# Low parts of 36 last-layer weights, made in the SwiGLU before and read back from DRAM, in place of GpSimd subtractions

## The chip, the core and the metric

The program runs on one core of one Trainium2 chip. A core has TensorE (PE in the profile, with its weight loads as PEld), VectorE (DVE), ScalarE (ACT), GpSimd (POOL) and SyncE (SP), which here issues DMAs, and 16 DMA engines that move data between DRAM and the on-chip SBUF. Every engine works through its own list of instructions in order; an instruction waits until the semaphores that it names have been raised. The metric is the device time of one execution in microseconds (us).

## The reference

Two layers of a block with four token mixers side by side, on 256 latent and 256 context tokens, width 1024, in float32. What matters here, cut down:

```
for l in range(2):
    x = x + 0.5 * g1 * swiglu(modulate(rms_norm(x), sh1, sc1), w_gate, w_up, w_down)   # both layers: latent and context
    y, yc = token_mixers(...)              # MLA, GLA, GQA, Hyena; then
    #   y = (sum over branches i of sigmoid(u @ w_gates_i) * (out_i @ w_branch[i])) @ w_out
    x = x + g2 * y
    x = x + 0.5 * g3 * swiglu(modulate(rms_norm(x), sh3, sc3), ...)                    # layer 1: latent tokens only
return rms_norm(x) * final_g
```

Hyena takes its three inputs from `u @ w_dp` (1024 to 1536 columns, 12 tiles of 128). The branch gates take `u @ w_gates` (4 x 1024 columns, 32 tiles of 128), the branch products `out_i @ w_branch[i]` (512 to 1024).

## The kernel before

**Split arithmetic.** A float32 product is made of three reduced ones. Each weight tile (128 partitions x 1024 float32, 512 KB) is loaded by SP into one of three raw buffers `wr` (`raw`, L318). `pieces` (L328) cuts it into two pieces of 512 columns. For each piece ScalarE writes the rounded high part `wh` (L311) and a second engine writes the rest, `wl = wr - wh` (L312). There are 8 buffers of each, so four weights can lie split ahead of TensorE. `mm3` (L303) then issues three matmuls per 128-column block: `wh` with the high part of the activation, `wh` with its low part, `wl` with its high part. The subtraction runs on VectorE, except where `self.share` is set: there GpSimd makes it (L335).

**Stages.** Layer 0 ends with its second SwiGLU on all 512 tokens (`ffn`, L586, called at L1408): three groups of 8, 8 and 6 hidden tiles, in each first the gate and up products (`gu`, two weights per hidden tile), then eight `dn` products. After each hidden tile or `dn` tile `side()` runs one step of other work; here that is 16 rows of the next layer's modulation (`ada_rows`, L453: one 512 KB load and two VectorE products with the conditioning row). Layer 1 runs its first SwiGLU, then the mixers for 256 latent tokens (`mixer`, L1339): first MLA and GQA, woven with the projections (`prep`). Then comes **the stage of this change** (L1357): Hyena and GLA are woven as two chains of high priority, and the merges of branches 0 (MLA) and 2 (GQA) fill in between them. Its weights are 12 `w_dp` tiles (for the three Hyena inputs, L1188), 8 `w_br` and 16 `w_gate` tiles (L1299, L1303), 36 in all, 72 pieces. In this stage `share` is 1, so all 72 subtractions are GpSimd's. The merges of branches 3 and 1 and the output product follow, with VectorE subtractions.

**What sets the order.** A tile scheduler fixes the order of each engine's instructions when the program is built, from priorities (`first`, `evac`, `ahead`) and its own costs. Pools hand out buffers in rotation; a tile that takes a buffer over waits for its last reader. SP's DMAs stand in one list, so a DMA that waits holds up those behind it.

Of the kernel before, what the change touches and what calls it, by code (L numbers as in the profile page):

```python
# [8 lines left out]
F32 = mybir.dt.float32  # L9
F32R = mybir.dt.float32r  # L10
# [7 lines left out]
P = 128  # L18
D = 1024
KD = 8  # L20
L = 256
NT = 512
DEPTH = 2
# [31 lines left out]
AHEAD = 200  # L55
EVAC = 400

SHARE_W = 1


PHASES = {"first": {"fh": 11, "fl": 9, "hp": 8, "aw": 6, "cb": 2},
# [158 lines left out]
class Net:  # L220
    def __init__(self, ctx, tc, A, out):
        self.tc, self.nc, self.A, self.out = tc, tc.nc, A, out
        pool = lambda n, b, **k: ctx.enter_context(tc.tile_pool(name=n, bufs=b, **k))
        self.const = pool("const", 1)
        self.sm = pool("sm", 2)
        self.up = pool("up", 1)
        self.wr = pool("wr", 3)
        self.wh = pool("wh", 8)
        self.wl = pool("wl", 8)
        self.fixed = {k: pool(k, b) for k, b in (("t", 6), ("m", 3), ("v", 8))}  # L230
        self.acc = (pool("acc0", 2, space=PSUM), pool("acc1", 2, space=PSUM))
        self.sps = pool("sps", 2, space=PSUM)
        self.tps = pool("tps", 2, space=PSUM)
        self.scopes = [ctx.enter_context(ExitStack()), ctx.enter_context(ExitStack())]
        self.dram = pool("dr", 1, space=bass.MemoryType.DRAM)
        self.mod = {}
        self.ahead = 0
        self.piece = 0
        self.share = 0
        self.begun = []  # L240

    def phase(self, name, sub=None):
# [77 lines left out]
        self.nc.sync.dma_start(out=r[:rows, :n], in_=ap)  # L320
        return r

    def weights(self, ap, n, rows=P, piece=512):

        with self.tc.high_priority(offset=-self.ahead):
            return self.pieces(self.raw(ap, n, rows), n, rows, min(piece, n))

    def pieces(self, r, n, rows, piece):  # L328
        parts = []
        for o in range(0, n, piece):  # L330
            m = min(piece, n - o)
            h = self.wh.tile([P, 512], F32R, tag="wh", name="wh")
            l = self.wl.tile([P, 512], F32R, tag="wl", name="wl")
            self.piece += 1
            eng = self.nc.gpsimd if self.share and self.piece % self.share == 0 else None  # L335
            self.two(h[:rows, :m], l[:rows, :m], r[:rows, o:o + m], eng)
            parts.append((h, l))

        def at(c, m):
            h, l = parts[c // piece]  # L340
            c %= piece
            return h[:rows, c:c + m], l[:rows, c:c + m]

        return at
# [238 lines left out]
            self.fm(p, w, u, n, ks=range(KD // 2))  # L583
            self.begun.append((w, p))

    def ffn(self, l, f, u, n, gt, filler=(), rows=()):  # L586
        nc, A = self.nc, self.A
        filler = list(filler)
        rows = self.rows(rows)

        def side():
            if filler:
                filler.pop(0)()
            else:
                next(rows, 0)

        for g0, g1 in GROUPS:
            hs = []
            for j in range(g0, g1):
                ps = []  # L600
                for e in range(2):
                    if self.begun:
                        w, p = self.begun.pop(0)
                        self.fm(p, w, u, n, ks=range(KD // 2, KD))
                    else:
                        w = self.weights(A["gu"][l, f, j, e], 1024)
                        p = self.psa(e, "gu")
                        self.fm(p, w, u, n)
                    ps.append(p)
                t = self.t("ft")  # L610
                nc.scalar.activation(t[:, :n], ps[0][:, :n], AF.Tanh, scale=0.5)
                nc.vector.scalar_tensor_tensor(out=t[:, :n], in0=t[:, :n], scalar=1.0, in1=ps[0][:, :n],
                                               op0=ALU.add, op1=ALU.mult)
                nc.vector.tensor_mul(t[:, :n], t[:, :n], ps[1][:, :n])
                h, lo = self.pair("fh", "hh", n, "fl")
                self.two(h[:, :n], lo[:, :n], t[:, :n])
                hs.append((h, lo))
                side()
            if gt.__class__ is tuple:
                gt = self.gate(*gt)  # L620
            q = g1 - g0
            for m in range(KD):
                w = self.weights(A["dn"][l, f, m, :, g0 * P:g1 * P], q * P)
                p = self.psa(m % 2, "dn")
                for j in range(q):
                    self.mm3(p[:, :n], w(j * P, P), (hs[j][0][:, :n], hs[j][1][:, :n]),
                             j == 0, j == q - 1)
                self.resid(p, m, n, gt)
                side()
        for _ in rows:  # L630
            pass

    def rows(self, pairs):
        if pairs:
            self.crow = [self.ld(self.tl("cb", "crow", D), self.cb[s]) for s in range(2)]
        for l, i in pairs:
            yield from self.ada_rows(l, i)

    def resid(self, p, m, n, gt):
        for s in range(n // L):  # L640
# [541 lines left out]
    def hyena(self, l, u, nseq, out):  # L1182
        nc, A = self.nc, self.A
        n = nseq * L

        def conv(i, z):
            p = self.psa(1, "dp")
            self.fm(p, self.weights(A["w_dp"][l, i], 1024), u, n)  # L1188
            w = [self.v["sw"][:, l * 36 + j * 12 + i:l * 36 + j * 12 + i + 1] for j in range(3)]
            nc.scalar.activation(z[:, :n], p[:, :n], AF.Identity, scale=w[1],  # L1190
                                 bias=self.v["sb"][:, l * 12 + i:l * 12 + i + 1])
            z3, p3 = (x[:, :n].rearrange("p (s t) -> p s t", t=L) for x in (z, p))
            nc.vector.scalar_tensor_tensor(out=z3[:, :, 1:], in0=p3[:, :, :L - 1], scalar=w[0], in1=z3[:, :, 1:],
                                           op0=ALU.mult, op1=ALU.add)
            nc.vector.scalar_tensor_tensor(out=z3[:, :, :L - 1], in0=p3[:, :, 1:], scalar=w[2], in1=z3[:, :, :L - 1],
                                           op0=ALU.mult, op1=ALU.add)

        src = self.packed("hv", "hv", n, 4)
# [10 lines left out]
        for i in range(2 * nseq):  # L1209
# [3 lines left out]
            h, lo = self.tl("o", "zth", 512, F32R), self.tl("o", "ztl", 512, F32R)  # L1213
# [3 lines left out]
        for od in range(2):  # L1217
# [6 lines left out]
            if od:  # L1224
                dst = [self.pair("o", "od", n) for _ in range(4)]
            nz = []
            for s in range(nseq):

                z = []
                for e in range(2):  # L1230
                    p = [self.half(F, 2 * e + k, zt[2 * s + k], "Z") for k in range(2)]
# [9 lines left out]
                a, b, c, d = z  # L1241
# [52 lines left out]
    def merge(self, l, b, ob, u, n, first=False, last=None):  # L1294
        nc, A = self.nc, self.A
        if first:
            self.y = self.packed("y", "y", n, KD)
        for mp in range(4):
            wb = self.weights(A["w_br"][l, b, mp], 1024)  # L1299
            for e in range(2):  # L1300
                m = 2 * mp + e
                pg = self.psa(0, "gate")
                self.fm(pg, self.weights(A["w_gate"][l, b * KD + m], 1024), u, n)  # L1303
                t = self.tl("m", "mt")
                if n == NT:
                    nc.scalar.activation(t[:, :n], pg[:, :n], AF.Tanh, scale=0.5)
                    p = self.psa(1, "br")
                else:
                    p = pg[:, n:]
                for k in range(4):  # L1310
                    self.mm3(p[:, :n], wb(e * 512 + k * P, P), (ob[k][0][:, :n], ob[k][1][:, :n]), k == 0, k == 3)
                with self.evac():
                    if n < NT:
                        nc.scalar.activation(t[:, :n], pg[:, :n], AF.Tanh, scale=0.5)
                    y = self.y[m]
                    nc.vector.scalar_tensor_tensor(out=y if first else t[:, :n], in0=t[:, :n], scalar=1.0, in1=p[:, :n],  # L1316
                                                   op0=ALU.add, op1=ALU.mult)
                    if not first:
                        nc.vector.tensor_add(y, y, t[:, :n])  # L1319
                if last is not None:  # L1320
                    h, lo = self.pair("yh", "yh", n, "yl")
                    self.two(h[:, :n], lo[:, :n], y)
                    last.append((h, lo))
                yield
# [14 lines left out]
    def mixer(self, l, u, last):  # L1339
# [4 lines left out]
        if last:  # L1344
# [3 lines left out]
                next(prep)  # L1348
            self.weave([self.mla(l, nq, oa), self.gqa(l, nq, oc)], prep)
            self.phase("end", "end2")  # L1350
            self.share = SHARE_W

            def merges():
                yield from self.merge(l, 0, oa, u, n, first=True)
                yield from self.merge(l, 2, oc, u, n)

            self.weave([self.hyena(l, u, nseq, od), self.gla(l, nq, ob)], merges())  # L1357
            self.share = 0
            for _ in self.merge(l, 3, od, u, n):
                pass  # L1360
        else:
# [14 lines left out]
    def run(self):  # L1376
# [14 lines left out]
        for l in range(DEPTH):  # L1391
# [13 lines left out]
            self.phase("ffn")  # L1405
            u = self.norm(*self.gain(l, 2), n)
            self.ada(l, 8)
            self.ffn(l, 1, u, n, (l, 2, 0.25), (), [] if last else later(l + 1, 0, 1))  # L1408
            if not last:
                u = self.norm(*self.gain(l + 1, 0), NT)  # L1410
        self.norm(self.v["final_g"], None, L)
# [21 lines left out]
```

## Time and profile before

| | |
|---|---|
| median of three runs | 2608.75 us (lowest 2604.82) |
| profiled execution | 2601.85 us, its span 2600.1 us |
| PE busy | 2497.5 us, 96% of the span |
| DVE, ACT, POOL busy | 1696.6, 1091.1, 264.9 us |
| DMA | 369.01 MB, mean 142 GB/s, 42.8% of 16 engines |
| TensorE's granted clock, mean | 0.986 |

The page cuts the span into 40 slices of 65 us. The second SwiGLU of layer 0 fills about 1173 to 1505 us, slices 18 to 23; the stage of the change about 2053 to 2292 us, slices 31 to 35. A digit is a busy share in tenths. All DMAs of the program were issued by SP (queue q1, `hardware_dynamic`); POOL issued none.

### The profile page before, as it was taken

Reading aid. Unit: us, or ns where it says so; the run is one execution under the profiler, and the core shown is the slowest. Engines: PE = TensorE matmul, PEld = TensorE weight load, DVE = VectorE, ACT = ScalarE, POOL = GpSimd, SP = SyncE. Lnnn points to the kernel's source line nnn. Section 1 sums busy time; section 2 is a strip of 40 time slices with the busy share of each in tenths; the row PEclk is TensorE's granted clock in tenths of the full one; section 3 lists DMA queues with packets and bytes.
Section 4 is the critical chain, followed back from the end, with each engine's and each line's share of the span. In section 5 each row is a group of like instructions: output and inputs, shape, how many; then the busy total and the mean of one; then the engine's idle time right before and its main releaser. Section 6 shows DMA issues by size and latency. Waiting matters only on the chain. (4 is left out here: it accounts for less than half of the span.)

```text
span 2600.1 us, 36866 instructions
## 1 busy us (share of the span) xinstructions
PE 2497.5 (96%) x13624; PEld 2058.8 (79%) x13624; DVE 1696.6 (65%) x3377; ACT 1091.1 (42%) x2127; POOL 264.9 (10%) x240
## 2 busy tenths in 40 slices
PE   6999999999999999999999999999999987899998
PEld 4778887887877667777888878888888777788998
DVE  5667858577547778746744466767458667776665
ACT  4333223333545554433232343232346664455554
POOL 2110003001000000020000030000020147401000
PEclk9999999999999999999999999999999999899999
DMA  7564535332313123245623244545353333356554
GB/s 253 176 213 170 190 128 192 134 108 100 126 57 122 61 88 106 89 156 174 205 97 97 86 158 146 178 146 174 102 187 130 114 120 122 114 161 210 177 184 124
DMA packets 122371, 369.01 MB, mean 142 GB/s; under 512 B 14090, under 2 KB 19660, under 8 KB 122192
## 3 DMA queue, kind: packets, MB, share of 16 engines
q1 hardware_dynamic: 122192, 366.66, 42.8%
q8 instruction: 107, 1.75, 0.3%
q14 instruction: 72, 0.59, 0.1%
HBM read 346.16 MB, written 20.45 MB: 141 GB/s over the span
## 5 line engine op out<-in xcount | busy, mean ns | idle before, releaser
L311 ACT CAST wh<-wr 128x512 fp32r<-128x512 f32 (+1 forms) x926 | 564.0, 613 | 1070.3 <-PE gu L301 396.0
L312 DVE TENSOR_TENSOR wl<-wr,wh 128x512 fp32r<-128x512 f32 (+1 forms) x854 | 577.1, 682 | 410.1 <-ACT wh L311 399.3
L301 PE MATMUL gu<-ul,wh 128*128 128x512 f32 (+1 forms) x1408 | 514.7, 366 | 2.5 <-DVE ul L542 2.5
L301 PE MATMUL gu<-uh,wh 128*128 128x512 f32 (+1 forms) x1408 | 512.3, 366 | 2.4 <-ACT uh L536 2.3
L301 PE MATMUL gu<-uh,wl 128*128 128x512 f32 (+1 forms) x1408 | 511.5, 364 | 1.3 <-DVE wl L312 1.3
L301 PE MATMUL dn<-hh,wh 128*128 128x512 f32 (+1 forms) x1408 | 389.5, 363 | 0.0
L301 PEld LDWEIGHTS gu<-ul,wh 128*128 128x128 f32 x1408 | 265.7, 189 | 58.4 <-DVE ul L542 9.3
L301 PEld LDWEIGHTS gu<-uh,wh 128*128 128x128 f32 x1408 | 265.8, 189 | 52.0 <-ACT uh L536 7.2
L301 PEld LDWEIGHTS gu<-uh,wl 128*128 128x128 f32 x1408 | 265.6, 189 | 44.0 <-DVE wl L312 1.7
L301 PEld LDWEIGHTS dn<-hh,wh 128*128 128x128 f32 x1408 | 252.6, 188 | 41.3
L301 PE MATMUL dn<-hh,wl 128*128 128x512 f32 (+1 forms) x704 | 255.3, 363 | 0.0
L502 POOL TENSOR_TENSOR nacc<-nacc,sq 128x512 f32<-128x512 f32 (+1 forms) x39 | 46.2, 1185 | 1745.1 <-ACT sq L500 1736.7
L301 PE MATMUL gate<-uh,wh 128*128 128x256 f32 (+1 forms) x768 | 202.3, 328 | 3.3 <-DVE y L1316 3.3
L464 DVE SCALAR_TENSOR_TENSOR aj<-aw,crow 128x1024 bf16<-128x1024 f32 x160 | 193.7, 1224 | 0.0
L301 PE MATMUL gate<-uh,wl 128*128 128x512 f32 (+1 forms) x512 | 177.0, 346 | 4.3 <-POOL wl L312 2.8
L301 PEld LDWEIGHTS dn<-hh,wl 128*128 128x128 f32 x704 | 132.3, 188 | 20.4
L301 PEld LDWEIGHTS gate<-uh,wh 128*128 128x128 f32 x768 | 132.0, 195 | 15.4 <-DVE y L1316 3.5
L301 PE MATMUL tm<-wh,uh 128*128 128x256 f32 x576 | 140.3, 288 | 1.6 <-ACT uh L536 1.0
L312 POOL TENSOR_TENSOR wl<-wr,wh 128x512 fp32r<-128x512 f32 x72 | 106.4, 1489 | 239.9 <-ACT wh L311 234.1
L301 PE MATMUL tm<-wl,uh 128*128 128x256 f32 x432 | 124.1, 287 | 0.0
L301 PEld LDWEIGHTS gate<-uh,wl 128*128 128x128 f32 x512 | 99.1, 194 | 15.9 <-POOL wl L312 3.0
L642 DVE SCALAR_TENSOR_TENSOR x<-dn,gt,x 128x256 f32<-128x256 f32 x168 | 74.4, 478 | 54.6 <-PE dn L301 54.6
(408 smaller groups left out, 3975.7 us busy)
## 6 DMA issues: line engine op xcount, KB each, us to landing
wr<-in_gu SPq DMA_DIRECT2D x176, 512.0 KB, 3.5
aw<-in_adat SPq DMA_DIRECT2D x80, 512.0 KB, 3.6
wr<-in_dn SPq DMA_DIRECT2D x64, 512.0 KB, 3.6
wr<-in_w_gate SPq DMA_DIRECT2D x64, 512.0 KB, 3.5
aw<-in_ada SPq DMA_DIRECT2D x48, 512.0 KB, 4.6
wr<-in_w_tm SPq DMA_DIRECT2D x36, 512.0 KB, 3.6
wr<-in_w_br SPq DMA_DIRECT2D x32, 512.0 KB, 3.5
wr<-in_dn SPq DMA_DIRECT2D x32, 384.0 KB, 3.2
```

Of the source, the lines that this page charges most:

```text
L301: self.nc.tensor.matmul(out, l, r, start=start, stop=stop)
L311: self.nc.scalar.copy(h, src)
L312: (eng or self.nc.vector).tensor_sub(l, src, h)
L464: nc.vector.scalar_tensor_tensor(out=x, in0=w, scalar=1.0, in1=self.crow[s], op0=ALU.mult, op1=ALU.mult, accum_out=o[:, s:s + 1])
L502: (nc.vector if first and k % 2 else nc.gpsimd).tensor_add(acc[:, :n], acc[:, :n], sq[:, :n])
L642: self.nc.vector.scalar_tensor_tensor(out=self.x[m][:, c], in0=p[:, c], scalar=gt[:, m, s:s + 1], in1=self.x[m][:, c], op0=ALU.mult, op1=A ...
```

## The change

`LOWS` lists the 36 weights of the stage, in the order in which they are needed. In layer 0's second SwiGLU each step of `side()` also runs `low_part` for one of them: SP loads the weight into a 1024-column buffer of the pool `aw` (5 buffers, shared with the modulation rows), ScalarE and VectorE split it as usual, and SP stores the two low pieces (256 KB each) to a DRAM tile. In the `dn` half of a group `side()` leaves the modulation rows alone as long as weights remain in the list. In the stage, `pieces` still loads the raw weight and lets ScalarE make `wh`; `wl` is now filled by a DMA that GpSimd issues from the DRAM tile. GpSimd's subtractions are gone, with `share` and `SHARE_W`.

```diff
+L1 = DEPTH - 1
+LOWS = tuple([(L1, "w_dp", i) for i in (8, 9, 10, 11)]
+             + [k for mp in range(4) for k in ((L1, "w_br", 0, mp), (L1, "w_gate", 2 * mp), (L1, "w_gate", 2 * mp + 1))]
+             + [(L1, "w_dp", i) for i in range(8)]
+             + [k for mp in range(4) for k in ((L1, "w_br", 2, mp), (L1, "w_gate", 16 + 2 * mp),
+                                               (L1, "w_gate", 17 + 2 * mp))])
...
-    def pieces(self, r, n, rows, piece):
+    def pieces(self, r, n, rows, piece, low=None):
         parts = []
         for o in range(0, n, piece):
             m = min(piece, n - o)
             h = self.wh.tile([P, 512], F32R, tag="wh", name="wh")
             l = self.wl.tile([P, 512], F32R, tag="wl", name="wl")
-            self.piece += 1
-            eng = self.nc.gpsimd if self.share and self.piece % self.share == 0 else None
-            self.two(h[:rows, :m], l[:rows, :m], r[:rows, o:o + m], eng)
+            if low is not None:
+                self.nc.scalar.copy(h[:rows, :m], r[:rows, o:o + m])
+                self.nc.gpsimd.dma_start(out=l[:rows, :m], in_=low[:rows, o:o + m])
+            else:
+                self.two(h[:rows, :m], l[:rows, :m], r[:rows, o:o + m])
             parts.append((h, l))
...
-        def side():
+        def side(low_only=False):
             if filler:
                 filler.pop(0)()
-            else:
+            elif not (low_only and lows):
                 next(rows, 0)
+            if lows:
+                self.low_part(lows.pop(0))
...
                 self.resid(p, m, n, gt)
-                side()
+                side(True)
...
+    def low_part(self, key):
+        src = self.A[key[1]][(key[0], *key[2:])]
+        w = self.ld(self.tl("aw", "lw", 1024), src)
+        dst = self.low[key] = self.dram.tile([P, 1024], F32, name="low" + "_".join(str(x) for x in key))
+        for o in (0, 512):
+            h, lo = self.t("lwh", F32R), self.t("lwl")
+            self.two(h, lo, w[:, o:o + 512])
+            self.nc.sync.dma_start(out=dst[:, o:o + 512], in_=lo)
...
-            self.fm(p, self.weights(A["w_dp"][l, i], 1024), u, n)
+            self.fm(p, self.weights(A["w_dp"][l, i], 1024, key=(l, "w_dp", i)), u, n)
...
-            self.share = SHARE_W
...
-            self.share = 0
...
-            self.ffn(l, 1, u, n, (l, 2, 0.25), (), [] if last else later(l + 1, 0, 1))
+            self.ffn(l, 1, u, n, (l, 2, 0.25), (), [] if last else later(l + 1, 0, 1), () if last else LOWS)
```

How the scheduler lays it out is seen at three places. First **GpSimd's list in the stage**, before (`yv` is a product of Hyena, `wl<-wr,wh` a subtraction):

```order
L763 MEMSET krp 128x64 x4
L312 TENSOR_TENSOR wl<-wr,wh 128x512 x48
L1245 TENSOR_TENSOR yv<-za,H 128x512
L1245 TENSOR_TENSOR yv<-zb,H 128x512
L312 TENSOR_TENSOR wl<-wr,wh 128x512 x24
L1245 TENSOR_TENSOR yv<-za,H 128x512
L1245 TENSOR_TENSOR yv<-zb,H 128x512
```

and with the change (the start of the stage, and the rows around its first `yv`):

```order
L782 MEMSET krp 128x64 x4
L341 DMA wl<-low_w_dp_10975 128x512 x2
L341 DMA wl<-low_w_br_0_11367 128x512 x2
L341 DMA wl<-low_w_gate_11465 128x512 x2
...
L341 DMA wl<-low_w_gate_12947 128x512 x2
L341 DMA wl<-low_w_gate_12997 128x512 x2
L1264 TENSOR_TENSOR yv<-za,H 128x512
L1264 TENSOR_TENSOR yv<-zb,H 128x512
L341 DMA wl<-low_w_dp_12553 128x512 x2
```

72 DMA issues stand where 72 subtractions stood; 46 of them, where 48 were, come ahead of the first `yv`.

Second, **SP's list in the SwiGLU**, at the end of the first group's `gu` products, before:

```order
L320 DMA wr<-in_dn 128x1024
L289 DMA aw<-in_adat 128x1024
L320 DMA wr<-in_dn 128x1024 x2
L289 DMA aw<-in_adat 128x1024
L320 DMA wr<-in_dn 128x1024 x2
```

and with the change:

```order
L324 DMA wr<-in_dn 128x1024
L293 DMA lw<-in_w_br 128x1024
L656 DMA low_w_gate_11465<-lwl 128x512 x2
L293 DMA lw<-in_w_gate 128x1024
L324 DMA wr<-in_dn 128x1024 x2
L293 DMA lw<-in_w_gate 128x1024
L656 DMA low_w_gate_11563<-lwl 128x512 x2
L293 DMA lw<-in_w_br 128x1024
L324 DMA wr<-in_dn 128x1024 x2
```

Between the loads of the SwiGLU's own weights (`wr`) now stand loads and stores of the low parts; a store waits for VectorE's `lwl`, and the next `wr` load stands behind it.

Third, **ScalarE's list at the last hidden tile of the first group**, with the change (`ft` and `hh` belong to the hidden tile, `lwh` to a low part):

```order
L620 ACTIVATE ft<-gu 128x512
L315 CAST lwh<-lw 128x512
L315 CAST wh<-wr 128x512
L315 CAST lwh<-lw 128x512 x3
L315 CAST wh<-wr 128x512
L315 CAST hh<-ft 128x512
L315 CAST lwh<-lw 128x512
L315 CAST wh<-wr 128x512
L315 CAST lwh<-lw 128x512 x3
L315 CAST wh<-wr 128x512
L315 CAST lwh<-lw 128x512 x4
```

Before, the same piece was `ft`, two casts of `wh`, `hh`, and 18 casts of `wh` in a row. Four casts of low parts now stand between `ft` and `hh`, and the low parts of the `dn` half crowd at its beginning. TensorE's own list is the same up to the late mixers; from there on gates and Hyena products come in another order.

## Rows read from the trace of the kernel before

**Rows 1.** The page: busy time of TensorE, and its granted clock in tenths, 40 slices.

```profile
PE 2497.5 (96%) x13624; PEld 2058.8 (79%) x13624; DVE 1696.6 (65%) x3377; ACT 1091.1 (42%) x2127; POOL 264.9 (10%) x240
PEclk9999999999999999999999999999999999899999
```

**Rows 2.** Busy time by stretch; last columns: granted clock, DMA share, GB/s.

```profile
core 0: us, PE busy (x) PEld busy (x) DVE busy (x) ACT busy (x) POOL busy (x), PEclk, DMA share, GB/s
1200.00:1300.00 100.00, 100.00 (x443) 82.81 (x442) 71.65 (x136) 28.82 (x48) 0.00 (x0) 1.00 0.56 184
1300.00:1400.00 100.00, 100.00 (x443) 82.84 (x442) 43.06 (x67) 31.95 (x53) 0.00 (x0) 1.00 0.30 95
2100.00:2180.00 80.00, 68.35 (x500) 60.94 (x500) 55.71 (x106) 41.29 (x80) 48.38 (x33) 0.96 0.44 141
2180.00:2200.00 20.00, 12.34 (x97) 11.87 (x96) 17.15 (x16) 10.83 (x21) 14.97 (x10) 0.82 0.30 99
2200.00:2260.00 60.00, 45.80 (x272) 39.47 (x271) 42.76 (x80) 24.77 (x46) 26.87 (x16) 0.84 0.34 106
2260.00:2292.00 32.00, 28.15 (x214) 24.85 (x212) 28.76 (x71) 14.63 (x30) 9.81 (x7) 0.98 0.24 79
2053.00:2292.00 239.00, 200.37 (x1362) 171.48 (x1359) 172.63 (x332) 123.03 (x256) 113.16 (x76) 0.93 0.37 119
2380.00:2400.00 20.00, 17.00 (x102) 10.81 (x101) 12.09 (x34) 8.83 (x16) 6.44 (x9) 0.91 0.80 288
```

**Rows 3.** TensorE's waits in 2053 to 2290: total us, times, longest.

```profile
PE AT L301 <- DVE ab L1015: 7.1, 2, 4.3
PE obT L348 <- DVE z L1071: 6.3, 3, 3.3
PE AT L301 <- issue: 4.3, 1, 4.3
PE gate L301 <- DVE y L1316: 3.3, 1, 3.3
PE dp L301 <- POOL wl L312: 3.2, 6, 0.8
PE gate L301 <- POOL wl L312: 2.8, 1, 2.8
...
PE AT L301 <- ACT zb L1233: 1.7, 1, 1.7
```

**Rows 4.** VectorE's groups in 2053 to 2290, four GLA heads: busy us, mean ns.

```profile
L1008 DVE TENSOR_TENSOR la<-ab 64x512 f32<-64x512 f32 x8 | 12.4, 1555 | 0.2
L1000 DVE TENSOR_TENSOR_SCAN ab<-scan,la 64x512 f32<-64x512 f32 x4 | 8.5, 2132 | 0.1
...
L998 DVE TENSOR_TENSOR_SCAN ab<-scan,la 64x512 f32<-64x512 f32 x4 | 6.8, 1704 | 0.1
```

**Rows 5.** The same instructions in layer 0, 860 to 1090, where GpSimd subtracts nothing.

```profile
L1008 DVE TENSOR_TENSOR la<-ab 64x512 f32<-64x512 f32 x8 | 5.5, 686 | 0.2
L1000 DVE TENSOR_TENSOR_SCAN ab<-scan,la 64x512 f32<-64x512 f32 x4 | 4.9, 1222 | 0.1
L998 DVE TENSOR_TENSOR_SCAN ab<-scan,la 64x512 f32<-64x512 f32 x4 | 4.8, 1212 | 0.1
```

**Rows 6.** GpSimd's subtractions, all 72: shortest, median, longest ns; first and last start.

```profile
L312 POOL TENSOR_TENSOR wl<-wr,wh x72: 1257/1292/5724, 2053.1 to 2268.5; 128x512 fp32r<-128x512 f32 x72
```

**Rows 7.** The two halves of a split in the SwiGLU, 1200 to 1500.

```profile
L312 DVE TENSOR_TENSOR wl<-wr,wh 128x512 fp32r<-128x512 f32 x108 | 74.1, 688 | 85.5 <-ACT wh L311 85.5
L311 ACT CAST wh<-wr 128x512 fp32r<-128x512 f32 x107 | 66.6, 623 | 196.9 <-PE gu L301 101.8 <-PE dn L301 61.7 <-issue 28.8
```

**Rows 8.** DMAs of 256 KB pieces, a store and a read-back: us from issue to landing.

```profile
xd<-x SPq DMA_DIRECT2D x16, 256.0 KB, 2.6
H<-hs SPq DMA_DIRECT2D x16, 256.0 KB, 4.3
```

**Rows 9.** SP's time to issue a weight load: shortest, median, longest ns.

```profile
L320 SPq DMA_DIRECT2D wr<-in_gu x176: 327/328/825, 17.9 to 2552.9; - x176
```

More of the change, by code (lines that the diff above doesn't have):

```diff
@@ L56 @@
 EVAC = 400
-SHARE_W = 1
+L1 = DEPTH - 1
[4 more added lines that the diff above has]
+                                               (L1, "w_gate", 17 + 2 * mp))])
 PHASES = {"first": {"fh": 11, "fl": 9, "hp": 8, "aw": 6, "cb": 2},
@@ L237, in __init__ @@
         self.ahead = 0
-        self.piece = 0
-        self.share = 0
+        self.low = {}
         self.begun = []
@@ L321, in raw, with weights @@
         return r
-    def weights(self, ap, n, rows=P, piece=512):
+    def weights(self, ap, n, rows=P, piece=512, key=None):
         with self.tc.high_priority(offset=-self.ahead):
-            return self.pieces(self.raw(ap, n, rows), n, rows, min(piece, n))
-    def pieces(self, r, n, rows, piece):
+            return self.pieces(self.raw(ap, n, rows), n, rows, min(piece, n), self.low.get(key))
+    def pieces(self, r, n, rows, piece, low=None):
         parts = []
@@ L584, in begin, with ffn @@
             self.begun.append((w, p))
-    def ffn(self, l, f, u, n, gt, filler=(), rows=()):
+    def ffn(self, l, f, u, n, gt, filler=(), rows=(), lows=()):
         nc, A = self.nc, self.A
         filler = list(filler)
-        rows = self.rows(rows)
-        def side():
+        rows, lows = self.rows(rows), list(lows)
+        def side(low_only=False):
             if filler:
                 filler.pop(0)()
-            else:
+            elif not (low_only and lows):
                 next(rows, 0)
+            if lows:
+                self.low_part(lows.pop(0))
         for g0, g1 in GROUPS:
@@ L1298, in merge @@
         for mp in range(4):
-            wb = self.weights(A["w_br"][l, b, mp], 1024)
+            wb = self.weights(A["w_br"][l, b, mp], 1024, key=(l, "w_br", b, mp))
             for e in range(2):
@@ L1302, in merge @@
                 pg = self.psa(0, "gate")
-                self.fm(pg, self.weights(A["w_gate"][l, b * KD + m], 1024), u, n)
+                self.fm(pg, self.weights(A["w_gate"][l, b * KD + m], 1024, key=(l, "w_gate", b * KD + m)), u, n)
                 t = self.tl("m", "mt")
@@ L1357, in mixer @@
             self.weave([self.hyena(l, u, nseq, od), self.gla(l, nq, ob)], merges())
-            self.share = 0
             for _ in self.merge(l, 3, od, u, n):
```

## The prediction, as it was put on record

> **What bounds the kernel now.** I read the page first. TensorE is busy for 96% of the span and its granted clock dips in one place, slices 33 and 34 [rows 1]: nothing off TensorE's path can be worth much, and what can be had lies where it idles. The second view is busy time by stretch [rows 2]. In the SwiGLU that takes on the new work TensorE is busy 100 of 100 us, so there is nothing to win there and only something to lose. In the stage that gets rid of work, 2053 to 2292, it is busy for 200.4 of 239 us: 38.6 us idle. The third view, its waits in that stage, says what ended the idle time [rows 3]. Only 3.2 + 2.8 = 6.0 us ended with a subtraction of GpSimd's. The rest ended with the serial chains of GLA and Hyena, above all the decay chain of a GLA head on VectorE before its `AT` products (7.1, 4.3 and 1.7 us, four waits for four heads). So the subtractions as such hardly hold TensorE up.
>
> But they hold VectorE up. The fourth view sets the same VectorE instructions in this stage [rows 4] beside layer 0, where GpSimd does not subtract [rows 5]: `la` 1555 ns against 686, the two scans 2132 against 1222 and 1704 against 1212. GpSimd's subtractions suffer as well, 1.26 us at the shortest and 5.7 at the longest [rows 6]. Shapes are equal, so the stretch is contention between the two engines.
>
> **The change, part by part.**
>
> *GpSimd's 72 subtractions go.* The 6.0 us of waits for them go with them. The stretch of the three VectorE groups goes: 8 x 0.869 + 4 x 0.910 + 4 x 0.492 = 12.6 us, 3.1 us per head, all of it ahead of that head's `AT`. Of each `AT` wait I give back the smaller of the wait and 3.1 us: 2.8 and 3.1 (the two that make 7.1, the longer 4.3), 3.1 and 1.7. That is 10.7 us. Behind these waits the chain goes on to `obT` (6.3 us) and to the merge's `y` (3.3); I leave those and the Hyena waits as they are. Bounds: nothing, if another input of the same product is late by as much, and all 38.6 us. I take 6.0 + 10.7 = 16.7 us.
>
> *The clock follows.* TensorE's granted clock is 0.96, 0.82, 0.84 and 0.98 in the four stretches [rows 2]. With two levels, 1.2 and 2.4 GHz, the time at the lower one is twice what is missing to 1: 6.4 + 7.2 + 19.2 + 1.3 = 34.1 us. Each dip lies in or behind idle time. TensorE was busy for 0.85, 0.62, 0.76 and 0.88 of those stretches, so about 25.7 us of its work ran at the lower level and would take half as long at the higher: 12.9 us. Bounds: nothing and 12.9. I take the share of the idle time that goes, 16.7 of 38.6: 5.6 us.
>
> *36 weights are split in the SwiGLU.* ScalarE gets 72 casts of 0.623 us, 44.9 us, VectorE 72 subtractions of 0.688 us, 49.5 us [rows 7], SP 36 loads and 72 stores of 0.33 us, 35 us [rows 9]. TensorE does 443 matmuls in 100 us, 0.226 us each, so a weight of 24 matmuls lasts 5.4 us and the 36 steps last about 300 us. ScalarE was busy for some 30 of 100 us and VectorE for 43 to 72, and the modulation rows that made the 72 are now spread over two groups; both have room. The cover is the lead of TensorE's weights: four split and three raw, 7 x 5.4 = 38 us. If it were gone, each late weight would cost up to 5.4 us. Behind SP's waiting stores stand the `wr` loads; a store waits for a cast and a subtraction, 1.3 us, and lands 2.6 us after its issue [rows 8], far less than the lead. On ScalarE `hh` of a group's last hidden tile stands behind four casts of low parts, 2.5 us; TensorE asks for it after 21 `dn` matmuls, 4.7 us. DMA: 37.7 MB more. In a `dn` half that is 1.57 MB per 5.4 us, 291 GB/s; the heaviest stretch of this kind in the trace ran at 288 GB/s with a DMA share of 0.80. Here the transfers have no reserve, but the lead bridges a half. Bounds: 0, and 10 us (a landing of 4.3 us late at each of two group ends). I take 2 us, near the lower end, since the row of 100 us without a gap is the nearest.
>
> *Low parts are read back.* The trace has no DMA of GpSimd's. A read-back of the same size from DRAM landed in 4.3 us when SP issued it [rows 8]; before, a piece was ready one cast and one subtraction after its buffer came free, 1.9 us. The 8 buffers of `wl` cover 8 x 12 matmuls of 0.13 us (214 in 28.15 us), 12.6 us, so the longer way is hidden as long as issues keep up. An issue costs GpSimd between 0.33 us (SP's) and 5.7 us (its longest subtraction). I take a value near SP's, since both are issues: 72 of them are some 24 to 90 us in the 215 us between the first and last subtraction. Cost: 1 us, bounds 0 and the rival below. The two products `yv` stand behind these issues as they stood behind subtractions. The raw buffers now come free after the cast alone, which can only help.
>
> **Sum.** -16.7 - 5.6 + 2 + 1 = -19.3 us on the profiled execution's 2601.85: 2582.5. Two of the runs of before lie 3 and 7 us above that execution, so I add 5: **2587 us**, 0.8% under the median of 2608.75. What a measurement of this kernel can tell from no change is about 2%, 52 us.
>
> **The rivals.**
>
> *The chain keeps its length.* VectorE's instructions shorten, but the waits move to the next late input (a table load or an exponential on ScalarE, `obT`, Hyena's `y`), and the new order of gates and Hyena products has gaps of its own. Only the 6.0 us for weights go, less 3 of cost: 2599, as a run 2604. For it speaks that one `AT` wait of 4.3 us ended in "issue" and one with ScalarE [rows 3]; against it, that the stretch sits in the chain itself. Chance 0.21.
>
> *The whole stage closes up.* All 38.6 us and 12.9 us of clock, less 3: 2553, as a run 2558. For it: gates are plentiful as fill, and VectorE is eased in Hyena's products too, which I left out. Against it: four heads and two Hyena orders stay serial. Chance 0.12, a third of it beyond 2%.
>
> *The SwiGLU pays.* If transfers in a `dn` half run at the 184 GB/s of the stretch with modulation rows, its 12.6 MB take 68 us in place of 43. Twice 25 us, less one lead of four split weights (22 us), is 28 us: 2587 + 26 = 2613. For it: the crowding of low parts at the start of the `dn` half and SP's blocked list. Against it: 288 GB/s has been seen. Chance 0.08.
>
> *GpSimd's issues become the bound of the stage* (the rival on the slower side). If GpSimd could prepare a DMA only while VectorE leaves it the way, it has 239 - (172.6 - 12.6) = 79 us for its 76 instructions there [rows 2], 72 of them issues. Up to 1.0 us each nothing happens. Beyond that the stage grows by 72 us for each further microsecond: at the shortest subtraction, 1.26 us, by 19, which uses up the gain (2606); from 2.1 us on the kernel is over 2% slower (2587 + 79 = 2666). For it: the two engines visibly block each other [rows 4 to 6]. Against it: an issue reads no tile. The Trainium skill, SBUF — State Buffer, section "Who interferes with whom", has a rule of this kind: descriptors of a GpSimd-issued DMA are made on GpSimd's cores, which are shut out while VectorE holds the shared port pair in a 2-port mode (copies, casts, products with a scalar), though not by an instruction with two tensors. The section before it gives 620 ns alone and about 3100 beside such a copy; by that, an estimate, 72 issues would take 223 us and the stage about 150 us more. No row here shows a GpSimd issue. Chance 0.09, 0.05 of it beyond 2%.
>
> **How the numbers follow.** My forecast has 0.50 and spans about 2570 to 2600 by its own bounds. Faster by over 2% is the far part of the closed-up stage: 0.04. Slower by over 2% is 0.05 of the issues and 0.01 of the SwiGLU: 0.06. Within 2%: 0.90. From 2560 to 2625 the range takes in the forecast, the unchanged chain, most of the SwiGLU case and parts of the others, 0.82 together.
>
> **What would show it.** In the changed profile: `la` at L1008's place near 690 ns and the scans near 1.22 us in the stage; no wait of TensorE for `wl` above 1 us; the sum of `AT` waits at 2 to 3 us; the granted clock in slices 33 and 34 at 0.9 or more; the SwiGLU at 100 of 100 us. Wrong would be: `wl` DMAs that land later than 12 us after their buffer came free, GpSimd issues above 1 us in VectorE's shadow, idle TensorE at the beginning of a `dn` half, or idle time in the stage that has only changed its releaser.

## The result, and the profile after

The changed kernel takes **2582.12 us** (median of five runs, 2579.11 to 2591.43), the kernel before on the same chip 2604.82: ratio **0.992, 95% interval 0.989 to 0.995**. That is 0.8%: inside the 2% that the prediction called no change, but the interval leaves no change out. (The ratio is taken over the runs in the fast state, without one run of the kernel before that took 11988.71 us and had also lifted the median of three at the start to 2608.75; the two medians alone would give 0.991.) The profiled execution of the changed kernel spans 2579.1 us, that of before 2600.1.

The page's rows that answer to [rows 1]:

```profile
PE 2490.8 (97%) x13624; PEld 2054.9 (80%) x13624; DVE 1713.3 (66%) x3449; ACT 1129.0 (44%) x2199; POOL 195.7 (8%) x240
...
PEclk9999999999999999999999999999999998999999
```

TensorE's share rose by a point, and one slice of the clock still shows 8 tenths: it is slice 33 now, where it was 34. The granted clock is 0.89 from 2100 to 2180 us, 0.83 to 2200 and 0.94 to 2260, where [rows 2] had 0.96, 0.82 and 0.84. The dip came earlier; it did not go.

I cut both traces at the same two events, the first `dp` product and the first `wo` product. Between them lie the same 1918 or 1919 matmuls in both. (This stretch is longer than the 239 us of [rows 2], since it also holds the gates behind the last head.) The view is busy time by stretch with the columns of [rows 2]. Before:

```profile
2053.50:2359.70 306.20, 267.20 (x1919) 238.37 (x1918) 220.65 (x420) 159.36 (x326) 112.73 (x76) 0.94 0.42 136
```

After, with two stretches of the SwiGLU ahead of it, which answer to the first two of [rows 2]:

```profile
1200.00:1300.00 100.00, 100.00 (x443) 82.80 (x442) 69.08 (x122) 42.53 (x74) 0.00 (x0) 1.00 0.81 278
1300.00:1400.00 100.00, 100.00 (x443) 82.81 (x442) 74.20 (x130) 44.75 (x78) 0.00 (x0) 1.00 0.73 251
2047.50:2336.80 289.30, 264.49 (x1918) 238.08 (x1917) 194.71 (x419) 159.69 (x326) 43.17 (x75) 0.95 0.67 209
```

The stage went from 306.2 to 289.3 us, 16.9 shorter: TensorE idles 24.8 us in place of 39.0 (-14.2), and its work takes 264.5 in place of 267.2 (-2.7, the clock). The SwiGLU is still full, 443 matmuls in each 100 us, though the DMA share rose from 0.56 to 0.81. VectorE does its 420 instructions of the stage (the second cut holds 419) in 194.7 us in place of 220.7. The rest of the 21 us of span lies ahead of the stage (6.0, since it begins at 2047.5 in place of 2053.5) and behind it (1.9 given back). I don't put what lies ahead down to the change: in the profiles of all kernels here the stage begins anywhere from 2047.5 to 2057.4 us, with TensorE's clock at its lower level in different places on the way.

TensorE's waits in the stage, in answer to [rows 3]:

```profile
PE dp L305 <- DMA wl<-low_w_dp: 8.0, 5, 3.2
PE obT L355 <- DVE z L1090: 5.1, 2, 3.5
PE dp L305 <- DVE STl L1072: 2.4, 1, 2.4
PE gate L305 <- DMA wl<-low_w_gate: 1.8, 2, 0.9
PE gate L305 <- DVE y L1335: 1.6, 1, 1.6
...
PE AT L305 <- DVE ab L1034: 1.4, 1, 1.4
PE AT L305 <- issue: 1.2, 1, 1.2
```

The `AT` waits fell from 13.1 to 2.6 us. The waits for low parts did not go: 6.0 us for GpSimd's subtractions became 9.8 us for DMAs, most of them `dp`'s. VectorE's groups, in answer to [rows 4] (busy us, mean ns), are where [rows 5] had them, but for `la`:

```profile
L1027 DVE TENSOR_TENSOR la<-ab 64x512 f32<-64x512 f32 x8 | 7.9, 985 | 0.2
L1019 DVE TENSOR_TENSOR_SCAN ab<-scan,la 64x512 f32<-64x512 f32 x4 | 4.9, 1221 | 0.1
L1017 DVE TENSOR_TENSOR_SCAN ab<-scan,la 64x512 f32<-64x512 f32 x4 | 4.9, 1214 | 0.1
```

One of the eight `la` took 3.07 us, the median is 0.69. The timeline (start, us; the `la` row holds two of them, 0.7 and 3.1) shows what ran beside it, the first two of the four products `yv` that are left to GpSimd:

```profile
2177.98 3.79 DVE L1027 TENSOR_TENSOR la<-ab 64x512 f32<-64x512 f32 x2
2178.67 1.31 POOL L1264 TENSOR_TENSOR yv<-za,H 128x512 f32<-128x512 f32 x1
2179.92 1.28 POOL L1264 TENSOR_TENSOR yv<-zb,H 128x512 f32<-128x512 f32 x1
```

The other two, from 2246.30, met a product of Hyena on VectorE in the same way, one of the two in this group (3.45 us, the other 0.68):

```profile
L1265 DVE TENSOR_TENSOR yw<-za,H 128x512 f32<-128x512 f32 x2 | 4.1, 2066 | 0.0
```

Together the two stretches are 5.2 us.

GpSimd's issues of the read-backs (shortest, median, longest ns) were short and even, VectorE busy or not:

```profile
L341 POOL DMA_DIRECT2D wl<-low_w_gate x32: 527/527/535, 2067.9 to 2245.8; - x32
L341 POOL DMA_DIRECT2D wl<-low_w_dp x24: 527/530/761, 2046.5 to 2218.9; - x24
```

What GpSimd's issues waited for (2050 to 2340; total us, times, longest) were buffers whose last readers had not run yet:

```profile
POOL wl L341 <- PE dp L305: 75.4, 21, 10.0
POOL wl L341 <- PE gate L305: 66.9, 35, 6.5
```

The transfers of the stage (2040 to 2290; the last column is us from issue to landing) crowd each other. The raw weights landed in 3.5 to 3.8 us before:

```profile
wr<-in_w_gate SPq DMA_DIRECT2D x25, 512.0 KB, 5.1
wl<-low_w_gate POOLq DMA_DIRECT2D x32, 256.0 KB, 5.0
...
wl<-low_w_dp POOLq DMA_DIRECT2D x24, 256.0 KB, 3.7
wl<-low_w_br POOLq DMA_DIRECT2D x16, 256.0 KB, 4.6
```

### The profile page after: what moved, and what is told of

Same layout as the page of the kernel before. It is cut to its first block, busy times and chain, and to the rows that moved or that the text cites. A ratio compares the mean times of both kernels' runs of the same rounds, so it can differ in the third digit from the quotient of the medians.

```text
span 2579.1 us, 37270 instructions
## 1 busy us (share of the span) xinstructions
PE 2490.8 (97%) x13624; PEld 2054.9 (80%) x13624; DVE 1713.3 (66%) x3449; ACT 1129.0 (44%) x2199; POOL 195.7 (8%) x240
## 4 chain that ended last, share of the span: by engine, by line
PE 51%; DVE 4%; DMA 2%; issue 2%; ACT 1%; POOL 1%; POOLq 0%; SPq 0%; DVEq 0%; ACTq 0%
PE gu L305 23%; PE dn L305 12%; PE gate L305 5%; PE wo L305 3%; PE tm L305 1%; DMA wl<-low_w_dp 1%; PE ada L305 1%; PE dp L305 1%; PE br L305 1%; PE S L305 1%; PE O L305 1%; POOL uy L544 1%; PE PT L355 1%; DVE wl L316 0%; PE Og L305 0%
## 5 line engine op out<-in xcount | busy, mean ns | idle before, releaser
L315 ACT CAST wh<-wr 128x512 fp32r<-128x512 f32 (+1 forms) x854 | 519.0, 613 | 961.6 <-PE gu L305 385.2
L305 PE MATMUL tm<-wh,ul 128*128 128x256 f32 x416 | 107.9, 286 | 0.0
L305 PEld LDWEIGHTS tm<-wh,uh 128*128 128x128 f32 x576 | 102.3, 193 | 6.8 <-ACT uh L543 2.8
```

What stands on the lines that cost most here:

```text
L305: self.nc.tensor.matmul(out, l, r, start=start, stop=stop)
L315: self.nc.scalar.copy(h, src)
```

## The experiments

My theory: the gain arises in the stage alone and comes from the end of the contention between GpSimd and VectorE; the SwiGLU takes its work for nothing; the read-back costs part of it. Rivals: the SwiGLU pays, the waits for the subtractions were what counted, or the load of the transfers eats the gain. "Stage" is the stretch from the first `dp` to the first `wo`, in one execution of each kernel; the changed kernel's two profiles differ by 0.8 us in it (289.3, and 290.1 in e12). All twelve kernels, each against the kernel before on the same chip:

| kernel | median us | ratio, 95% interval | stage | TensorE idle in it |
|---|---|---|---|---|
| before (profile) | 2604 to 2606 | 1 | 306.2 | 39.0 |
| e1 split in both | 2605.2 | 1.000, 0.998 to 1.002 | 306.6 | 38.0 |
| e2 no SwiGLU part | 2587.5 | 0.993, 0.991 to 0.995 | 288.0 | 27.3 |
| e3 no read-back | 2565.3 | 0.985, 0.982 to 0.987 | 271.6 | 11.6 |
| e4 VectorE subtracts | 2591.8 | 0.995, 0.993 to 0.996 | 296.4 | 26.0 |
| e5 subtractions unread | 2599.8 | 0.999, 0.998 to 1.000 | 303.7 | 33.4 |
| e6 read-back unread | 2575.2 | 0.989, 0.987 to 0.991 | 277.9 | 20.4 |
| e7 dp on VectorE | 2582.3 | 0.991, 0.989 to 0.993 | 283.0 | 20.7 |
| e8 SP issues | 2578.0 | 0.990, 0.988 to 0.991 | 280.7 | 20.2 |
| e9 bfloat16 low parts | 2574.3 | 0.988, 0.987 to 0.990 | 279.1 | 20.1 |
| e10 dp by SP | 2585.7 | 0.992, 0.991 to 0.994 | 286.4 | 22.9 |
| e11 SP, dp on VectorE | 2578.4 | 0.990, 0.988 to 0.992 | 278.8 | 17.5 |
| e12 changed, again | 2585.6 | 0.993, 0.991 to 0.994 | 290.1 | 26.5 |

**e1, the SwiGLU part alone.**

```diff
-                self.nc.scalar.copy(h[:rows, :m], r[:rows, o:o + m])
-                self.nc.gpsimd.dma_start(out=l[:rows, :m], in_=low[:rows, o:o + m])
+                self.two(h[:rows, :m], l[:rows, :m], r[:rows, o:o + m], self.nc.gpsimd)
```

> The SwiGLU does all of its new work (36 loads, 72 casts, 72 subtractions, 72 stores), but the stage splits its weights itself, with the 72 subtractions on GpSimd as in the kernel before; nothing is read back. Theory (the gain arises in the stage alone, from the end of the contention between GpSimd and VectorE and of the waits for GpSimd's subtractions, and the SwiGLU takes its work for nothing): the time of the kernel before, 2605 us, ratio to it 0.998 to 1.003; in the stage la near 1.5 us and AT waits near 13 us; TensorE 100 of 100 us in the SwiGLU from 1200 to 1500. Rival 'the SwiGLU pays and the stage gains more than is seen': 2612 us or more. Rival 'part of the gain arises outside the stage' (up to 6 us of the profiled difference stands ahead of it): 2599 us or less.

Ratio 1.000, and the stage is that of before, `AT` waits and all (7.1 + 4.9 + 1.7 us). So what the SwiGLU's 72 casts, subtractions and stores cost, and what is gained outside the stage, is less than the interval can show, some 4 us either way.

**e2, the stage part alone.**

```diff
+            self.low = {k: self.A[k[1]][(k[0], *k[2:])] for k in LOWS}
...
-            self.ffn(l, 1, u, n, (l, 2, 0.25), (), [] if last else later(l + 1, 0, 1), () if last else LOWS)
+            self.ffn(l, 1, u, n, (l, 2, 0.25), (), [] if last else later(l + 1, 0, 1), ())
```

> The SwiGLU does nothing new; in the stage the low parts are read back as in the changed kernel, but from the raw weights in DRAM in place of stored low parts (so the low part of 36 weights is replaced by the weight itself). Theory: the time of the changed kernel, 2582 us, give or take 4, since the SwiGLU's work lies beside TensorE's. Rival 'the SwiGLU pays': below 2576. Waits for the read-back near 10 us as in the changed kernel either way; AT waits 2 to 3 us.

The ratio is the changed kernel's (0.993 against 0.992 and 0.993); its microseconds are 1.5 above my band. From the other side too, the SwiGLU pays nothing that shows. Waits for the read-back are 12.7 us.

**e3, neither subtraction nor read-back.**

```diff
-            l = self.wl.tile([P, 512], F32R, tag="wl", name="wl")
+            l = h if low is not None else self.wl.tile([P, 512], F32R, tag="wl", name="wl")
...
-                self.nc.gpsimd.dma_start(out=l[:rows, :m], in_=low[:rows, o:o + m])
```

> The SwiGLU makes and stores the low parts as in the changed kernel; the stage neither subtracts nor reads back: the high part takes the low part's place in the matmuls of those 36 weights (so their low parts are left out of the result). It is the ceiling of any way to bring the low parts in. Theory 'the read-back costs the 9.8 us that TensorE waits for it, and something of the clock': 2568 to 2574, I take 2571 us. Rival 'these waits only stand in place of the next late input' (z, STl, y of the serial chains): 2579 to 2584. Rival 'the whole stage closes up': below 2562.

Below what the theory allowed: 2565. Its stretch and its longest waits:

```profile
2051.20:2322.80 271.60, 259.95 (x1919) 235.49 (x1918) 189.32 (x420) 159.18 (x326) 5.12 (x4) 0.96 0.48 153
```

```profile
PE obT L354 <- DVE z L1089: 3.3, 1, 3.3
PE dp L305 <- DVE STl L1071: 2.2, 1, 2.2
PE AT L305 <- DVE ab L1033: 2.0, 2, 1.8
```

Against the changed kernel the stage loses another 17.7 us, 13.2 of them idle, 4.5 in TensorE's work. That is what the read-back costs with all that hangs on it, nearly twice TensorE's waits for it. Part of it is VectorE's: the two stretched instructions above make 5.2 of the 5.4 us by which its work falls, from 194.7 to 189.3; here `la` and `yw` take 0.69 us at most. And 420 VectorE instructions take these 189.3 us where in the kernel before they took 220.7: the stretch was 31 us in all, not the 12.6 that I had counted.

**e4, VectorE subtracts, no DRAM.**

```diff
-SHARE_W = 1
+SHARE_W = 0
```

> The kernel before with its 72 subtractions of the stage on VectorE instead of GpSimd; no work in the SwiGLU, no read-back. VectorE was busy 172.6 us of the 239, of which 12.6 was stretch; with 72 x 0.688 = 49.5 us it comes to about 210. Theory 'contention alone makes the chains long': la near 0.7 us, but 50 us of subtractions in VectorE's queue hold up chains and weights instead, so part of the gain, 2590 to 2602 us, I take 2597. Rival 'only the contention counts, VectorE has room': 2580 to 2586, as the changed kernel. Rival 'VectorE's load is the bound': 2606 us or more, slower than before.

In the theory's range. `la` is at 687 ns, and the waits that come up are for casts and subtractions of a gate (3.5 and 3.4 us). Taking the subtractions off GpSimd, to the engine that it had disturbed, gives more than half of the change's gain (0.995 against 0.993, though the intervals overlap; 9.8 of 16.9 us of stage) with no DMA at all.

**e5, GpSimd subtracts, TensorE doesn't read it** (e1's edit, and this).

```diff
-            parts.append((h, l))
+            parts.append((h, h if low is not None else l))
```

> As the changed kernel in the SwiGLU; in the stage GpSimd makes its 72 subtractions as in the kernel before, but TensorE does not read them: the high part takes the low part's place in those matmuls (their low parts are left out). So the contention of GpSimd with VectorE stays whole, and the waits of TensorE for GpSimd are gone. Stage from the first dp to the first wo: 306.2 us in the kernel before, 271.6 without subtractions and read-back. Theory 'the contention is most of it': AT waits stay near 13 us, la near 1.5 us, the stage 295 to 302 us, time 2596 to 2602, I take 2599. Rival 'the waits for GpSimd's subtractions, with what they delay, are most of it': stage below 285 us, time 2584 or less.

2599.8, as the theory had it; the stage is 1.7 us above its band. Its stretch and its waits:

```profile
2050.80:2354.50 303.70, 270.29 (x1919) 243.11 (x1918) 220.62 (x419) 160.03 (x326) 105.27 (x76) 0.93 0.43 137
```

```profile
PE AT L305 <- DVE ab L1033: 7.5, 2, 5.3
PE AT L305 <- issue: 6.5, 2, 5.8
PE obT L354 <- DVE z L1089: 5.6, 3, 2.9
PE yi L305 <- ACT Yh L315: 4.3, 2, 2.3
PE Z L305 <- DVE ztl L316: 1.8, 1, 1.8
PE Z L305 <- ACT zth L315: 1.5, 1, 1.5
```

Without a single wait for `wl` only 2.5 us of stage are won: 5.6 of idle time, less 3.1 that TensorE's work takes longer, at a granted clock of 0.93. VectorE's work is that of the kernel before, 220.6 us. The other 32.1 us down to e3, where GpSimd does not subtract, are contention and the clock that goes with it (21.8 of idle time, 10.3 of TensorE's work): GLA's `AT` and `obT`, but also Hyena's `Z` and `yi`, which are all gone or shorter in e3.

**e6, read back but not read** (the edit of e5 on the changed kernel).

> As the changed kernel, the 72 read-backs included, but TensorE does not read what they bring: the high part takes the low part's place in those matmuls (their low parts are left out). So GpSimd's issues and the 18.9 MB of transfers stay, and the waits for their landing are gone. The stage is 289.3 us in the changed kernel, 271.6 without read-back. Theory 'the price of the read-back is TensorE's waits for its landing': stage 271 to 276 us, time 2564 to 2571, I take 2568. Rival 'its price is the load on the DMA engines (share 0.67 in place of 0.42 in this stage) and later raw weights': stage 281 to 288, time 2575 to 2581, with waits for wh or wr in place of those for the low parts.

The time is at the rival's lower edge, the stage between the two bands:

```profile
2054.20:2332.10 277.90, 257.53 (x1918) 233.01 (x1917) 189.30 (x419) 159.04 (x326) 42.98 (x75) 0.96 0.70 217
```

The stage is 289.3 - 277.9 = 11.4 us shorter than the changed kernel's, 4.4 of it idle time and 7.0 TensorE's work (the clock). The landing waits are not all that went: read-backs that nobody reads don't hold up GpSimd's list, its first `yv` starts at 2158.2 us in place of 2178.7, and no `la` or `yw` takes over 0.70 us. 6.3 us remain against e3: against e3's 2.2 us for `dp <- DVE STl` there is one such wait of 9.9 us; the waits for `wh` or `wr` that the rival expected did not come up (1.4 us, as in e3). ScalarE's waits show why:

```profile
ACT dfth L315 <- DMA wr<-in_dft: 12.9, 2, 8.0
```

VectorE stood with its list behind the split of this table, which landed late among read-backs that nothing held back here. So the split into 11.4 for the landing and 6.3 for the transfers is rough: in the changed kernel, where buffers hold the read-backs back, ScalarE waits 4.1 us for that table.

**e7, dp's low parts on VectorE** (the two lines of `w_dp` taken out of `LOWS`).

> The changed kernel with 24 low parts in place of 36: those of the two branches' gates and products are made in the SwiGLU and read back, those of the 12 dp weights are split in the stage, on VectorE (24 subtractions of 0.69 us, 16.5 us). In the changed kernel 8.0 of the 9.8 us of waits for the read-back are dp's. Theory: dp's waits go, the gates' (1.8 us) stay or shrink, VectorE with 155 + 16 of 230 us has room: stage 278 to 284 us, time 2571 to 2577, I take 2574, faster than both kernels. Rival 'VectorE's subtractions hold up the chains of GLA and Hyena by as much': 2580 to 2590, since with all 72 on VectorE it was 2592.

Its stage of 283.0 is in my band, its time is not: 0.991 is not to be told from the changed kernel. The `dp` waits went, and others came up in their place (`yi <- ACT Yh` 2.8, `pre <- DVE hv` 2.4, `gate <- DVE y` 2.4).

**e8, SP issues the read-backs.**

```diff
-                self.nc.gpsimd.dma_start(out=l[:rows, :m], in_=low[:rows, o:o + m])
+                self.nc.sync.dma_start(out=l[:rows, :m].bitcast(F32), in_=low[:rows, o:o + m])
```

> The changed kernel with the 72 read-backs issued by SP in place of GpSimd. Theory (what TensorE waits for is a transfer that starts only when a buffer of wl comes free and lands 3.7 to 5.0 us later; who issues it matters little): waits for the low parts of 6 to 14 us, time 2577 to 2588, I take 2583. Rival 'GpSimd's issues are the cost': 2572 or less. Rival 'SP's list blocks': the wr loads stand behind read-backs that wait for a buffer, so waits for wr and wh come up: 2592 or more.

The time is inside the theory's range, the reason was wrong: waits for low parts are 2.1 us, not 6 to 14. Two things differ from the changed kernel that may explain it. The read-backs of gates landed in 4.1 us (5.0 there). And GpSimd's list was free, so that its products ran when their input came and hit neither `la` nor `yw` (0.69 us at most):

```profile
2146.29 1.30 POOL L1264 TENSOR_TENSOR yv<-za,H 128x512 f32<-128x512 f32 x1 [222.19 <-DVE za L1253]
```

In the changed kernel that product stood behind issues that waited for buffers, until 2178.67. By time the two kernels are hardly apart: 0.988 to 0.991 here, 0.991 to 0.994 for the changed kernel in e12, 0.989 to 0.995 at first.

**e9, low parts in bfloat16.**

```diff
-        dst = self.low[key] = self.dram.tile([P, 1024], F32, name="low" + "_".join(str(x) for x in key))
+        dst = self.low[key] = self.dram.tile([P, 1024], mybir.dt.bfloat16, name="low" + "_".join(str(x) for x in key))
...
-            h, lo = self.t("lwh", F32R), self.t("lwl")
+            h, lo = self.t("lwh", F32R), self.t("lwl", mybir.dt.bfloat16)
```

> The changed kernel with the 36 low parts kept in DRAM as bfloat16: stores of 128 KB in place of 256, and read-backs by GpSimd that read half the bytes and write the same tiles. In the changed kernel TensorE's waits for the landing made 11.4 us of the stage (289.3 against 277.9 when nobody reads what lands) and the transfers beside other loads 6.3 us (277.9 against 271.6). Theory 'both shrink with the bytes read': landing 2.5 to 3.5 us in place of 3.7 to 5.0, stage 278 to 285 us, time 2572 to 2579, I take 2576. Rival 'what counts is that the transfer starts only when the buffer is free, and its fixed part': stage 286 to 292 us, time 2580 to 2586.

Of the kernels that leave no low part out, this has the lowest time: 0.988 against 0.993 of the changed kernel beside it (e12), their intervals apart. From e8 and e11, at 0.990, it is not to be told. Its stretch and waits:

```profile
2051.50:2330.60 279.10, 258.99 (x1919) 233.24 (x1918) 194.84 (x419) 160.18 (x326) 43.04 (x75) 0.97 0.71 217
```

```profile
PE dp L305 <- DMA wl<-low_w_dp: 3.4, 3, 1.3
PE gate L305 <- DMA wl<-low_w_gate: 2.5, 2, 1.3
```

Waits for low parts are 5.9 us against 11.9 in e12. The landings shortened less than I expected (3.4 to 4.4 us against 3.6 to 5.1), and the DMA engines' busy time did not shrink (0.71 x 279.1 = 198 us, 0.67 x 289.3 = 194 in the changed kernel). Half the bytes read is what was changed; by what way the landing gains is open. It is not by GpSimd's products: one `la` and one `yw` are stretched here too, to 3.07 and 3.45 us.

**e10, dp's read-backs by SP, the rest by GpSimd.**

```diff
+                if key[1] == "w_dp":
+                    self.nc.sync.dma_start(out=l[:rows, :m].bitcast(F32), in_=low[:rows, o:o + m])
+                else:
```

> The changed kernel with the 24 read-backs for dp issued by SP and the other 48 by GpSimd. With all 72 issued by SP the stage took 280.7 us and the waits for dp's low parts were gone. Theory 'on GpSimd's list dp's read-backs stood behind gates' that waited for their buffers': dp's waits for the low parts below 2 us in place of 8.0, stage 279 to 285 us, time 2575 to 2581, I take 2578. Rival 'GpSimd's issues as such are slow to land': dp's waits gone but those of gate above 4 us, stage 285 to 290. Rival 'two lists cross on one ring of buffers': waits of 8 us or more remain, 2582 or more.

The theory fell. `dp`'s waits went as expected, but one of 3.9 us for a gate's low part and 3.1 us of `Og <- DVE STl` came, and the time is the changed kernel's. The stage lies in the first rival's band (285 to 290), with the gate's wait just under the 4 us that this rival named. GpSimd's list still holds its first `yv` until 2175.2 us, and one `yw` takes 3.45. Whether it is GpSimd's landing or its blocked list that e8 avoids, this doesn't say.

**e11, e7 and e8 together.**

> Two of the earlier edits together: the low parts of dp's weights are split on VectorE in the stage (nothing of them is made in the SwiGLU), and the other 48 read-backs are issued by SP. Apart, the first gave a stage of 283.0 us, the second 280.7. Theory 'fewer transfers and a list without blocking add up': 276 to 281 us, time 2572 to 2579, I take 2576. Rival 'both remove the same waits (dp's for the low parts), so the second adds nothing, and VectorE's subtractions cost': 281 to 286 us, time 2578 to 2585.

In the band, with no wait for a read-back left and 17.5 us idle, but by time not to be told from e8. **e12, the changed kernel again:**

> The changed kernel as it is, beside the three versions of it. All theories expect the ratio of its first measurement, 0.992 to the kernel before within 0.003, and a stage of 287 to 291 us with waits for the low parts of 8 to 12 us, most of them dp's. A version that is really better than the changed kernel has an interval that does not reach this ratio.

As expected: 0.993, a stage of 290.1, waits for low parts of 8.9 + 3.0 us.

## Why the prediction was right, and where its sum was wrong

The time was forecast at 2587 us and came out at 2582; the working sum for the profiled execution was 2582.5, and that one took 2580.88. Contention was the right mechanism for the gain, but two terms were far off, in opposite directions. That the sum came out so close is luck.

- **Contention** was mis-sized. I counted the stretch of three groups, 12.6 us, all of it in the `AT` chain, and gave back 10.7 us; the `AT` waits did fall by 10.5. The step that failed is "I leave those and the Hyena waits as they are": the stretch was 31 us (220.7 against 189.3 us for 420 instructions in e3), and Hyena's splits and products got shorter with GLA's. Rows were at hand in the trace of the kernel before:

```profile
L1014 DVE TENSOR_TENSOR qd<-qd,e 128x256 f32<-128x256 f32 x4 | 4.1, 1025 | 0.1
L1247 DVE TENSOR_TENSOR za<-za,H 128x512 f32<-128x512 f32 x2 | 3.2, 1595 | 0.0
```

Twice the columns of `qd` take 0.69 us in layer 0; in e4, without GpSimd's subtractions, the two take 0.42 and 0.68 us.

- **The 6.0 us of waits for subtractions**: e5 takes them away and wins 5.6 us of idle time, but 2.5 of stage, since the clock took 3.1 back.
- **The read-back** was priced at 1 us and costs 17.7 us of stage (e3). The failing step is "the longer way is hidden": I set a landing of 4.3 us against a cover of 12.6 us, as if a buffer came free in the order of need. GpSimd's issues waited 75 and 67 us for buffers whose reader TensorE had not come to (above), and TensorE then waited 9.8 us for landings. The waiting issues also hold up the `yv` behind them, as the subtractions did, so that these still stretch two of VectorE's instructions. A free buffer alone does not explain it: in e8 SP issues into the same buffers, also waits 34 and 32 us for TensorE, and TensorE's waits are 2.1 us. Whether the order of the list or the way of issuing makes that difference is open.
- **Together**: -34.6 + 17.7 = -16.9 us of stage, where I had -16.7 - 5.6 + 1 = -21.3. **The clock** gave 2.7 us in the changed kernel, not 5.6; its dip moved to slice 33.
- **The SwiGLU** cost nothing that e1 and e2 can show, against the 2 us of the sum.
- **The 5 us** added for runs longer than the profiled execution rested on two runs and did not show: the changed kernel's median lies 1.2 us above its profiled run, though two of its five runs lie 9 and 11 above.

Of the signs, the scans (1.22 us), the sum of the `AT` waits (2.6) and the full SwiGLU came as written, `la` but for one. TensorE's longest wait for `wl` was 3.2 us, not below 1, and slice 33 shows 8 tenths. One sign of being wrong came true: the waits for subtractions changed their releaser and became waits for DMAs.

Of the rivals, "GpSimd's issues become the bound" is refuted by the rows: 0.53 us each, at most 0.76, 39 us in all. By the rule of the Trainium skill (SBUF — State Buffer, "Who interferes with whom") a VectorE instruction in a 2-port mode shuts descriptor making out; no issue here shows it. (The 620 and 3100 ns of that rival's estimate are, in the Trainium skill, the times of a whole DMA and not of its issue.) The same section says that a VectorE instruction with two SBUF inputs contends with a GpSimd instruction that reads SBUF; the `la` of 3.07 us beside `yv`, 0.69 elsewhere, agrees. "The whole stage closes up" did not come: 14 of the 39 idle us closed. Without the read-back it would have come nearer, 27 of the 39 (e3). "The chain keeps its length" is out by the `AT` waits, "the SwiGLU pays" by e1 and e2.

What stays open: the medians differ by 22.7 us here and 19.8 in e12, the stage by 16.9 and 16.1. The remaining 4 to 6 us lie within the spread ahead of the stage, and I can't assign them. In e3, e5 and e6 no matmul holds a buffer of low parts either, so that other work can run further ahead; a part of their gain may be that, and no run tells it apart.

## What to carry to other kernels

When two engines stretch each other, price the end of it by the busy time of all instructions in the stretch against the same ones elsewhere, not by those in the chain that you happen to watch. A read-back that replaces an on-chip operation can start only when its buffer is free and the issues ahead of it in the list are out, so look at who reads the buffer last, and at what stands behind the issue, before you call it hidden. Before a round trip through DRAM, try the operation on the other engine (here more than half the gain), and if the trip is made, try it narrow (bfloat16 low parts gave the lowest time, 0.988) and from another queue (0.990 with SP's).

## What was not expected of the hardware

- Two GpSimd products of 1.3 us stretch one VectorE instruction with two SBUF inputs from 0.69 to 3.07 us, and it ended 0.57 us behind the second of them: beside them VectorE seems to have got hardly anything done.
- A GpSimd issue of a DMA takes 527 ns at the median, SP's 327, and was hardly stretched while VectorE was busy for 195 of 289 us.
- Read-backs of half the source bytes kept the DMA engines busy as long (198 us in e9, 194 in the changed kernel), and still landed earlier (3.4 to 4.4 us against 3.6 to 5.1).
